# Four transformer layers and a mixed attention/SSM block on one core: new first loads, new POOL costs in the planner, a narrower rule for breaking small matmuls, and a longer search

## The chip, the cores and the metric

One Trainium2 chip, one core. The metric is the device time of one execution in microseconds, the median of several. Within the core, TensorE (PE, with its weight loads shown as PEld), VectorE (DVE), ScalarE (ACT), GpSimd (POOL) and the DMA queue that SyncE (SP) issues run beside one another and wait on semaphores.

## The reference

A sequence of 256 tokens of width 1024 goes through four layers and one further block, all in float32:

```
for i in range(4):
    hn = rms_norm(x, norm_gains[i, 0])
    m = diff_attention / stick_breaking_attention / sliding_window_sink_attention (hn)   # kinds 0, 1, 2, 0
    x = x + rms_norm(m, norm_gains[i, 1])
    f = swiglu(rms_norm(x, norm_gains[i, 2]), w_gate, w_up, w_down)                      # 1024 -> 2816 -> 1024
    x = x + rms_norm(f, norm_gains[i, 3])
xn = rms_norm_2(x, mix_norm)
z = xn @ w_in                                   # q, k, v, gate_a, u, gate_s
attn = dilated_mixture_attention(q, k, v) * silu(gate_a)
ssm  = s5_glu(u, ...) * silu(gate_s)            # 32 groups, 64 complex states each, a diagonal scan
h = x + concat(attn, ssm) @ w_out
h = h + sigmoid(rms_norm_2(h) @ w_ple_gate) * (p @ w_ple_proj)
```

Rope angles need sine and cosine of position times frequency; the SSM needs sine and cosine of its eigenvalues, and powers of them.

## The kernel before

The tokens are two blocks b of 128. A weight matrix is cut into chunks of 8 row tiles by 512 columns (2 MB). SP loads a chunk as raw tiles (three buffers of 1 MB). ACT copies it into a rounded half "hi", DVE subtracts to get "lo", and `gemm` (L726) sums three products per row tile (hi·hi, hi·lo, lo·hi), so one chunk is 24 matmuls of 512 columns for each b. The weight tiles w have eleven buffers, PSUM accumulators two for each b. The first chunk's raw tiles and the transposed input xT0 lie in the S8 ring (`S8`, L539), three buffers of 1 MB, which later holds q, k, v, the FFN accumulator and the two SSM preparation tiles pp and pt, in the order in which the program makes them. A new user of a buffer waits for the last use of the tile three places earlier: layer 1's k comes after pp.

Nothing is issued in program order. `_Program.record` (L234) keeps every instruction with a cost (`cost`, L208), its predecessors and the ring of its tiles. `schedule` (L461) then plans all engines together: `forward` (L320) is a list scheduler that starts, on the engine that is free first, the ready instruction of the lowest priority value; `backward` (L423) derives new priorities from the end. 24 tries of three passes with random settings are made, the plan with the earliest end wins, and `issue` (L491) writes the instructions out in that order, so every engine's queue is a fixed sequence. Before an activation whose function lies in another table set it issues a table load; Copy and Square need no set of their own.

What the change and the prediction touch:

- `cost`, L208: POOL's elementwise operations over n elements of each partition.
- `record`, L234: the delay put on each edge from one instruction to the next.
- `forward`, L320: with TensorE, an instruction of fewer than 100 columns is put off for a wide one when the columns of the current stretch of planned time are behind a pace; a run of instructions of one array tiling is kept together where possible.
- `setup`, L579: first loads, in the order `nc.head`; eight warm-up matmuls (`warm`, L610). After the head come the loads in `rope_tables` (L655), `prep_diff` (L960), `prep_sink` (L1116) and the block-two gains (L1618).
- `sincos`, L641: range reduction and Sin, once for the sine and once for the cosine.
- `ssm_prep_tasks`, L1291: on POOL, `coef` and `powers` are some hundred operations of 16 elements in one chain, then eight `part_e` sets of six operations of 256 elements; each ends in four transposes (tile eT) and eight small matmuls (tile ke) on TensorE. The last set's result goes out by a DMA, taps<-pp.
- `ssm_scan` and `ssm_y`, L1474 on: 128 matmuls S of 31 columns on half the array's columns, and 128 matmuls Y on a quarter of them.

All instructions of the program have the profile line L499, that of `issue`, so tiles tell them apart.

Of the kernel before, what the change touches and what calls it, by code (L numbers as in the profile page):

```python
# [10 lines left out]
F32 = mybir.dt.float32  # L11
# [61 lines left out]
CONST, COFF = _consts()  # L73

# [41 lines left out]
class _Program:  # L116
# [14 lines left out]
    DRAIN = 110.0  # L131
    window = 6
    tries, seed = 24, 346
# [74 lines left out]
    def cost(eng, method, args, kw):  # L208
# [23 lines left out]
        return 150 + (2.9 if op == ALU.mult else 3.5) * n  # L232

    def record(self, eng, method, args, kw):  # L234
# [41 lines left out]
        for o in preds.values():  # L276
            if o is not op:
                self.edge(o, op, 0.0 if o.eng == eng == "tensor" else o.lat)
# [41 lines left out]
    def forward(self, delta):  # L320
# [11 lines left out]
        while len(order) < len(self.ops):  # L332
            for e in dirty:
# [4 lines left out]
                for op in lst:  # L338
                    s = op.ready if op.ready > f else f
                    w = self.DMA[e][0] if op.call == "dma_start" else op.cost  # L340
                    if op.func is not None and self.set_of[op.func] != table:
                        w += self.SWITCH
# [18 lines left out]
                if e == "tensor" and best is not None and best.cols < 100:  # L361
# [45 lines left out]
            else:  # L407
                fin = s + op.cost
                if op.func is not None and self.set_of[op.func] != table:
                    table = self.set_of[op.func]  # L410
                    fin += self.SWITCH
# [49 lines left out]
    def schedule(self):  # L461

        self.ring_edges()
# [3 lines left out]
        self.log = []  # L467
        for i in range(self.tries):
# [8 lines left out]
            if not fresh and sigma:  # L477
                for o, z in zip(self.ops, rng.normal(0.0, sigma, len(self.ops))):
                    o.prio += z
            for _ in range(3):  # L480
                end, order = self.forward(delta)
                if best is None or end < best[0]:
                    best = (end, order, [o.start for o in self.ops])
                    self.log.append((i, round(end)))
                self.backward()
        self.end, order, starts = best
        for o, t in zip(self.ops, starts):
            o.start = t
        return order

    def issue(self, tc):  # L491
        order = self.schedule()
        table = None
        with tc.manual_schedule():
            for op in order:
# [10 lines left out]
class _Net:  # L506
# [72 lines left out]
    def setup(self):  # L579
# [3 lines left out]
        self.gT = cp.tile([P, 80], F32, name="gT")  # L583
# [6 lines left out]
        load(self.gT, a["gT"])  # L590
# [4 lines left out]
        n = len(nc.ops)  # L595
        self.prepped = 0
        if self.depth:
            self.prep(1)
        raws = [o for o in nc.ops[n:] if o.eng == "sync"]
        for b in range(NB):  # L600
            load(self.x[b], a["x"][0][b * P:(b + 1) * P, :])
        self.ident = cp.tile([P, P], F32, name="ident")
        load(self.ident, self.consts_dram[:, COFF["ident"][0]:COFF["ident"][0] + P])
        if raws:
            nc.head = [loads[1], raws[0], loads[0], raws[1], loads[2], raws[2], loads[3]] + raws[3:] + loads[4:]
        self.neghalf = cp.tile([P, 8], F32, name="neghalf")
        nc.vector.memset(self.neghalf, -0.5)
        self.warm(8)
# [32 lines left out]
    def sincos(self, sin_out, cos_out, ang, tmp):  # L641
        nc = self.nc
        for shift, dst in ((0.0, sin_out), (0.25, cos_out)):
            nc.vector.tensor_scalar(tmp, ang, 1.0 / TWO_PI, shift, op0=ALU.mult, op1=ALU.add)
            nc.vector.tensor_scalar(tmp, tmp, MAGIC, None, op0=ALU.add)
            nc.vector.tensor_scalar(tmp, tmp, MAGIC, None, op0=ALU.subtract)
            nc.vector.scalar_tensor_tensor(dst, tmp, -C1, ang, op0=ALU.mult, op1=ALU.add)
            nc.vector.scalar_tensor_tensor(dst, tmp, -C2, dst, op0=ALU.mult, op1=ALU.add)
            nc.vector.scalar_tensor_tensor(dst, tmp, -C3, dst, op0=ALU.mult, op1=ALU.add)
            if shift:  # L650
                nc.vector.tensor_scalar(dst, dst, math.pi / 2, None, op0=ALU.add)
            nc.vector.tensor_scalar(dst, dst, math.pi, -math.pi, op0=ALU.min, op1=ALU.max)
            nc.scalar.activation(dst, dst, AF.Sin)

    def rope_tables(self):  # L655
        nc, a, cp = self.nc, self.a, self.cp
        pt = self.pw(1, "post")
# [1186 lines left out]
```

## Time and profile before

| | |
|---|---|
| median of 3 runs | 1386.53 us (1385.73 to 1387.84) |
| the profiled execution | 1389.7 us |
| its span, first to last instruction | 1387.9 us |
| TensorE busy in the span | 1360.8 us |
| VectorE, ScalarE, GpSimd busy | 913.9, 766.2, 198.4 us |
| HBM | 236.90 MB read, 6.67 MB written, 175 GB/s over the span |
| mean granted TensorE clock | 0.998 |

The profiled execution is 1.8 us longer than its span, and 3.2 us above the median. TensorE's busy time is a union of modelled stretches: a matmul's stretch reaches past the start of the next, so short stops between matmuls hide in it, and a slow pace shows only in counts (matmuls in so many us). Idle time is told as the wait before an instruction, with what ended it.

### The profile page before, as it was taken

The page shows a single profiled execution, that of the slowest core. Times are in us where ns is not written, and L with a number is a line of the kernel's source. Part 1 is how long each engine was busy: PE and PEld are TensorE (multiplying, and loading weights), DVE is VectorE, ACT ScalarE, POOL GpSimd, SP SyncE. Part 2 cuts the span into 40 slices and gives each one's busy share as a digit, 9 for nine tenths or more (in the row PEclk, how much of TensorE's full clock was granted, in tenths as well). Part 3 has the DMA queues.
Part 4 walks back from the last instruction along what each step waited for, and adds up shares of the span by engine and source line. Part 5 has one row for each costly group of instructions (what it writes and reads, how often), then busy time and mean ns, then how long its engine had stood idle before and what let it go on. Part 6 is the DMA issues. An engine that isn't in the chain of part 4 may idle for free.

```text
span 1387.9 us, 17967 instructions
## 1 busy us (share of the span) xinstructions
PE 1360.8 (98%) x6820; PEld 1119.9 (81%) x6820; DVE 913.9 (66%) x1351; ACT 766.2 (55%) x1268; POOL 198.4 (14%) x331
## 2 busy tenths in 40 slices
PE   8999999999999999999999999999999999999998
PEld 5788887888888888788878888888888888887776
DVE  7986654758756655558966555598875464685583
ACT  6766554446877544446756544466664453564562
POOL 0011067603000059202000000010000000020000
PEclk9999999999999999999999999999999999999999
DMA  8553654656443566655525645554546474566550
GB/s 301 188 162 131 223 206 142 202 191 213 159 152 108 182 207 212 216 163 167 161 84 197 211 154 182 180 173 152 182 137 212 152 228 151 167 214 188 178 190 35
DMA packets 135510, 244.73 MB, mean 176 GB/s; under 512 B 6544, under 2 KB 28176, under 8 KB 135424
## 3 DMA queue, kind: packets, MB, share of 16 engines
q1 hardware_dynamic: 135424, 243.59, 53.3%
q8 instruction: 53, 0.87, 0.3%
q14 instruction: 33, 0.27, 0.1%
HBM read 236.90 MB, written 6.67 MB: 175 GB/s over the span
## 4 chain that ended last, share of the span: by engine, by line
PE 80%; DVE 8%; ACT 4%; POOL 4%; DMA 3%; issue 1%; SPq 0%; ACTq 0%; DVEq 0%; POOLq 0%
PE acc L499 70%; PE tr L499 3%; DVE w L499 3%; POOL pp L499 2%; DVE rp L499 1%; ACT w L499 1%; PE z L499 1%; PE sc L499 1%; DMA raw<-in_a_w_in_dram 1%; PE sS L499 1%; POOL pt L499 1%; PE o L499 1%; POOL q L499 1%; DMA raw<-in_w_ple_gate_dram 1%; PE Y L499 1%
## 5 line engine op out<-in xcount | busy, mean ns | idle before, releaser
L499 PE MATMUL acc<-w,hnT 128*128 128x512 f32 (+1 forms) x3552 | 837.2, 391 | 5.6 <-ACT w L499 3.1
L499 PEld LDWEIGHTS acc<-w,hnT 128*128 128x128 f32 x3552 | 653.5, 189 | 140.6 <-ACT w L499 4.2
L499 DVE TENSOR_TENSOR w<-raw,w 128x1024 fp32r<-128x1024 f32 (+1 forms) x431 | 518.9, 1218 | 185.1 <-ACT w L499 176.2
L499 ACT ACTIVATE w<-raw 128x1024 fp32r<-128x1024 f32 (+1 forms) x431 | 442.6, 1040 | 207.2 <-PE acc L499 165.9
L499 PE MATMUL acc<-w,hT 128*128 128x512 f32 x1056 | 252.0, 392 | 0.9 <-ACT hT L499 0.9
L499 PEld LDWEIGHTS acc<-w,hT 128*128 128x128 f32 x1056 | 196.0, 188 | 41.6 <-ACT hT L499 1.3
L499 PE MATMUL acc<-w,oT 128*128 128x512 f32 x480 | 120.5, 400 | 0.8 <-DVE oT L499 0.8
L499 PEld LDWEIGHTS acc<-w,oT 128*128 128x128 f32 x480 | 88.2, 188 | 19.9 <-DVE oT L499 1.2
L499 POOL TENSOR_TENSOR po_r<-po_v,neghalf 128x1 f32<-128x1 f32 x16 | 14.6, 910 | 532.0 <-DVE po_v L499 532.0
L499 DVE SCALAR_TENSOR_TENSOR sg<-acc,pn_r,sg 128x512 f32<-128x512 f32 (+1 forms) x48 | 33.8, 704 | 68.6 <-PE acc L499 49.2
L499 ACT ACTIVATE sg<-acc,pn_r 128x512 f32<-128x512 f32 (+1 forms) x48 | 31.1, 649 | 86.4 <-PE acc L499 86.4
L499 POOL TENSOR_TENSOR pg<-pg 128x128 f32<-128x128 f32 x96 | 60.6, 655 | 39.1 <-PE acc L499 35.9
L499 ACT ACTIVATE hT<-tr 128x512 fp32r<-128x512 f32 (+1 forms) x48 | 26.6, 555 | 58.6 <-PE tr L499 58.6
L499 DVE TENSOR_TENSOR hT<-tr,hT 128x512 fp32r<-128x512 f32 (+1 forms) x48 | 30.8, 641 | 24.7 <-ACT hT L499 24.7
L499 DVE TENSOR_TENSOR facc<-acc,facc 128x512 f32<-128x512 f32 x32 | 22.0, 687 | 32.8 <-PE acc L499 32.8
L499 POOL TENSOR_TENSOR pn_r<-pn_v,neghalf 128x1 f32<-128x1 f32 x20 | 16.4, 821 | 176.7 <-DVE pn_v L499 170.5
L499 ACT ACTIVATE ad_e<-sc,ad_nm 128x128 f32<-128x128 f32 (+1 forms) x64 | 26.2, 422 | 18.2 <-DVE ad_nm L499 15.3
L499 ACT ACTIVATE hnT<-gx 128x512 fp32r<-128x512 f32 x36 | 22.6, 628 | 24.4 <-DVE gx L499 24.1
L499 POOL TENSOR_TENSOR ad_r<-ad_v,neghalf 128x4 f32<-128x4 f32 x8 | 9.9, 1232 | 148.4 <-DVE ad_v L499 140.2
L499 DVE TENSOR_TENSOR hnT<-gx,hnT 128x512 fp32r<-128x512 f32 x36 | 25.2, 699 | 6.0 <-ACT hnT L499 5.7
L499 ACT ACTIVATE sqj<-x 128x512 f32<-128x512 f32 x40 | 24.9, 623 | 6.9 <-DVE x L499 6.7
L499 POOL TENSOR_TENSOR pt<-pp 128x256 f32<-128x256 f32 x32 | 25.2, 800 | 18.8 <-PE ke L499 18.2
(232 smaller groups left out, 1112.0 us busy)
## 6 DMA issues: line engine op xcount, KB each, us to landing
raw<-in_ffn_w_gate_dram SPq DMA_DIRECT2D x40, 1024.0 KB, 5.2
raw<-in_ffn_w_up_dram SPq DMA_DIRECT2D x40, 1024.0 KB, 5.1
raw<-in_ffn_w_down_dram SPq DMA_DIRECT2D x32, 1024.0 KB, 5.2
raw<-in_a_w_in_dram SPq DMA_DIRECT2D x22, 1024.0 KB, 5.2
raw<-in_ffn_w_down_dram SPq DMA_DIRECT2D x16, 768.0 KB, 4.5
raw<-in_b_w_in_dram SPq DMA_DIRECT2D x12, 1024.0 KB, 5.2
raw<-in_w_in_dram SPq DMA_DIRECT2D x12, 1024.0 KB, 5.2
raw<-in_a_w_out_dram SPq DMA_DIRECT2D x8, 1024.0 KB, 5.1
```

The costliest lines, as they stand in the source:

```text
L499: r = getattr(getattr(self.nc, op.eng), op.call)(*op.args, **op.kw)
```

## The change

- A new input "pack" (134 columns) replaces the input of the norm gains (80 columns). It also holds the positions, the rope frequencies, the two subln gains, the q and k gains and the sinks, which nine separate loads brought before.
- The head of the load queue also takes chunk 1: identity matrix, then both raw tiles of chunk 1, then x; before, x and the identity ended the head.
- 13 warm-up matmuls in place of 8.
- `issue` loads the first needed activation table ahead of everything, and the planner counts no switch for it.
- `sincos` works on sine and cosine side by side in one tile.
- POOL's cost becomes 340 + 1.85 n (multiply) or 340 + 2.8 n ns, where it was 150 + 2.9 n or 150 + 3.5 n.
- An edge from POOL to TensorE gets 3000 ns more.
- The rule that breaks small matmuls for wide ones holds only when TensorE's current tiling is the full array.
- The search has 60 tries of three passes (24 before), another seed, and then 120 single passes that put noise on the priorities within one stretch of 20, 60 or 150 us of the best plan and keep what does not end later.

The diff, cut to its core:

```diff
+PACK = 134
...
+    SPARE = 3000.0
...
-    tries, seed = 24, 346
+    tries, local, seed = 60, 120, 3
...
-        return 150 + (2.9 if op == ALU.mult else 3.5) * n
+        return 340 + (1.85 if op == ALU.mult else 2.8) * n
...
-                self.edge(o, op, 0.0 if o.eng == eng == "tensor" else o.lat)
+                lag = 0.0 if o.eng == eng == "tensor" else o.lat
+                self.edge(o, op, lag + self.SPARE if (o.eng, eng) == ("gpsimd", "tensor") else lag)
...
-                    if op.func is not None and self.set_of[op.func] != table:
+                    if op.func is not None and self.set_of[op.func] != table is not None:
...
-                if e == "tensor" and best is not None and best.cols < 100:
+                if e == "tensor" and best is not None and best.cols < 100 and mode in (None, (P, P)):
...
+                    fin += self.SWITCH if table is not None else 0.0
...
-                    fin += self.SWITCH
...
+        def attempt(i, delta):
+            nonlocal best
+            prio = [o.prio for o in self.ops]
+            end, order = self.forward(delta)
+            if best is None or end <= best[0]:
+                if best is None or end < best[0]:
+                    self.log.append((i, round(end)))
+                best = (end, order, np.array([o.start for o in self.ops]), np.array(prio), (delta, self.stick, self.pace))
...
-                end, order = self.forward(delta)
-                if best is None or end < best[0]:
-                    best = (end, order, [o.start for o in self.ops])
-                    self.log.append((i, round(end)))
+                attempt(i, delta)
...
-        self.end, order, starts = best
-        for o, t in zip(self.ops, starts):
+        for i in range(self.tries, self.tries + self.local):
+            width, sigma = rng.choice((20e3, 60e3, 150e3)), rng.choice((100.0, 300.0, 1000.0, 3000.0))
+            centre = rng.uniform(0.0, best[0])
+            delta, self.stick, self.pace = best[4]
+            near = np.abs(best[2] - centre) < width / 2
+            prio = np.where(near, best[2 + rng.integers(2)] + rng.normal(0.0, sigma, n), best[3])
+            for o, x in zip(self.ops, prio.tolist()):
+                o.prio = x
+            attempt(i, delta)
+        self.end, order, starts = best[:3]
+        for o, t in zip(self.ops, starts.tolist()):
...
-        table = None
+        table = next((self.set_of[op.func] for op in order if op.func is not None), None)
...
+            if table:
+                self.nc.scalar.preload_act_table_set(table)
...
-        self.gT = cp.tile([P, 80], F32, name="gT")
+        self.pack = cp.tile([P, PACK], F32, name="pack")
+        self.gT = self.pack[:, 0:80]
...
-        load(self.gT, a["gT"])
+        load(self.pack, a["pack"])
...
-        if self.depth:
-            self.prep(1)
-        raws = [o for o in nc.ops[n:] if o.eng == "sync"]
+        raws = [[], []]
+        for i in range(2 if self.depth else 0):
+            n = len(nc.ops)
+            self.prep(i + 1)
+            raws[i] = [o for o in nc.ops[n:] if o.eng == "sync"]
+        self.ident = cp.tile([P, P], F32, name="ident")
+        load(self.ident, self.consts_dram[:, COFF["ident"][0]:COFF["ident"][0] + P])
...
-        self.ident = cp.tile([P, P], F32, name="ident")
-        load(self.ident, self.consts_dram[:, COFF["ident"][0]:COFF["ident"][0] + P])
-        if raws:
-            nc.head = [loads[1], raws[0], loads[0], raws[1], loads[2], raws[2], loads[3]] + raws[3:] + loads[4:]
+        if self.depth:
+            r0, r1 = raws
+            nc.head = [loads[1], r0[0], loads[0], r0[1], loads[2], r0[2], loads[3]] + r0[3:] + loads[4:5] + r1[:2]
+            nc.head += loads[5:] + r1[2:]
...
-        self.warm(8)
+        self.warm(13)
...
-    def sincos(self, sin_out, cos_out, ang, tmp):
+    def sincos(self, out, ang, tmp):
...
-        for shift, dst in ((0.0, sin_out), (0.25, cos_out)):
-            nc.vector.tensor_scalar(tmp, ang, 1.0 / TWO_PI, shift, op0=ALU.mult, op1=ALU.add)
-            nc.vector.tensor_scalar(tmp, tmp, MAGIC, None, op0=ALU.add)
-            nc.vector.tensor_scalar(tmp, tmp, MAGIC, None, op0=ALU.subtract)
-            nc.vector.scalar_tensor_tensor(dst, tmp, -C1, ang, op0=ALU.mult, op1=ALU.add)
-            nc.vector.scalar_tensor_tensor(dst, tmp, -C2, dst, op0=ALU.mult, op1=ALU.add)
-            nc.vector.scalar_tensor_tensor(dst, tmp, -C3, dst, op0=ALU.mult, op1=ALU.add)
-            if shift:
-                nc.vector.tensor_scalar(dst, dst, math.pi / 2, None, op0=ALU.add)
-            nc.vector.tensor_scalar(dst, dst, math.pi, -math.pi, op0=ALU.min, op1=ALU.max)
-            nc.scalar.activation(dst, dst, AF.Sin)
+        for i in range(2):
+            nc.vector.tensor_scalar(tmp[:, i], ang, 1.0 / TWO_PI, 0.25 * i, op0=ALU.mult, op1=ALU.add)
+        nc.vector.tensor_scalar(tmp, tmp, MAGIC, None, op0=ALU.add)
+        nc.vector.tensor_scalar(tmp, tmp, MAGIC, None, op0=ALU.subtract)
+        nc.vector.scalar_tensor_tensor(out, tmp, -C1, ang[:, None, :].to_broadcast(list(out.shape)), op0=ALU.mult,
+                                       op1=ALU.add)
+        nc.vector.scalar_tensor_tensor(out, tmp, -C2, out, op0=ALU.mult, op1=ALU.add)
+        nc.vector.scalar_tensor_tensor(out, tmp, -C3, out, op0=ALU.mult, op1=ALU.add)
+        nc.vector.tensor_scalar(out[:, 1], out[:, 1], math.pi / 2, None, op0=ALU.add)
+        nc.vector.tensor_scalar(out, out, math.pi, -math.pi, op0=ALU.min, op1=ALU.max)
+        nc.scalar.activation(out, out, AF.Sin)
...
-        pt = self.pw(1, "post")
-        inv, pos = pt[:, 0:32], pt[:, 32:32 + NB]
-        posi = self.pw(1, "posi")[:, :NB].bitcast(I32)
-        o, n = COFF["inv"]
-        nc.sync.dma_start(out=inv, in_=self.consts_dram[:, o:o + n])
-        nc.sync.dma_start(out=posi, in_=a["positions"][0].rearrange("(b p) -> p b", p=P))
-        nc.vector.tensor_copy(pos, posi)
+        inv = self.pack[:, 82:114]
+        pos = self.pw(1, "pos")[:, :NB]
+        nc.vector.tensor_copy(pos, self.pack[:, 80:82].bitcast(I32))
...
-        self.sincos(sc[:, :64], sc[:, 64:128], ang[:, :64], tmp[:, :64])
+        two = lambda t: t[:, :128].rearrange("p (t n) -> p t n", t=2)
+        self.sincos(two(sc), ang[:, :64], two(tmp))
...
-        gcol = self.small(1, "gcol")
-        nc.sync.dma_start(out=gcol, in_=a["a_subln"][inst].rearrange("(p o) -> p o", o=1))
+        gcol = self.pack[:, 114 + inst:115 + inst]
...
-        sk = self.small(16, "sink")
-        nc.sync.dma_start(out=sk, in_=a["c_sinks"][inst].partition_broadcast(P))
+        sk = self.pack[:, 118:134]
...
-            mag, ai_, ar_, num, den, cr, ci, t1, t2 = (cols(16) for _ in range(9))
+            mag, num, den, cr, ci, t1 = (cols(16) for _ in range(6))
+            trig, t2 = (cols(32).rearrange("p (t g) -> p t g", t=2) for _ in range(2))
+            ai_, ar_ = trig[:, 0], trig[:, 1]
...
-            self.sincos(ai_, ar_, t1, t2)
+            self.sincos(trig, t1, t2)
...
-                for key, src, sc in (("gq", "q_norm_2", 0.125), ("gk", "k_norm_2", 1.0)):
-                    g = self.small(1, key)
-                    for h in range(2):
-                        nc.sync.dma_start(out=g[64 * h:64 * h + 64, :], in_=a[src][0].rearrange("(p o) -> p o", o=1))
-                    if sc != 1.0:
-                        g2 = self.small(1, key + "s")
-                        nc.vector.tensor_scalar(g2, g, sc, None, op0=ALU.mult)
-                        g = g2
-                    st[key] = g
+                st["gk"] = self.pack[:, 117:118]
+                st["gq"] = self.small(1, "gqs")
+                nc.vector.tensor_scalar(st["gq"], self.pack[:, 116:117], 0.125, None, op0=ALU.mult)
...
+    two = lambda v: np.tile(v[0], 2)[:, None]
+    pack = [rows.transpose(2, 0, 1).reshape(P, 80), i["positions"][0].reshape(NB, P).T.astype(np.int32).view(np.float32),
+            CONST[:, COFF["inv"][0]:COFF["inv"][0] + 32], i["a_subln"].T, two(i["q_norm_2"]), two(i["k_norm_2"]),
+            np.broadcast_to(i["c_sinks"][0], (P, 16))]
...
-        "gT": rows.transpose(2, 0, 1).reshape(P, 80),
+        "pack": np.concatenate(pack, axis=1),
...
```

## Rows read from the trace of the kernel before

**Rows 1.** The page, busy time of each engine and its share of the span.
```profile
PE 1360.8 (98%) x6820; PEld 1119.9 (81%) x6820; DVE 913.9 (66%) x1351; ACT 766.2 (55%) x1268; POOL 198.4 (14%) x331
```

**Rows 2.** Busy time by stretch: each engine, granted clock, DMA share, GB/s.
```profile
9.00:12.00 3.00, 3.00 (x9) 2.29 (x8) 2.63 (x7) 3.00 (x9) 0.00 (x0) 1.00 1.04 405
13.00:16.00 3.00, 3.00 (x15) 2.47 (x14) 3.00 (x6) 3.00 (x8) 0.00 (x0) 1.00 1.06 347
...
25.00:72.00 47.00, 46.30 (x231) 37.64 (x230) 46.02 (x83) 30.68 (x69) 0.00 (x0) 1.00 0.56 189
...
227.00:239.00 12.00, 9.49 (x34) 7.59 (x33) 3.24 (x7) 2.39 (x3) 8.50 (x16) 0.72 0.26 101
239.00:1255.00 1016.00, 1011.24 (x4966) 836.25 (x4965) 668.44 (x906) 566.54 (x911) 133.26 (x181) 1.00 0.54 176
1255.00:1345.00 90.00, 84.83 (x625) 68.60 (x625) 58.29 (x128) 45.45 (x71) 2.00 (x2) 1.00 0.56 180
```

**Rows 3.** The timeline of the first 26 us: start, length, what, wait before it.
```profile
0.98 3.59 PE L499 MATMUL warm<-warm 128*128 128x512 bf16 x8 [0.98 <-DVE neghalf L499]
...
5.10 1.28 ACT L499 ACT_TABLE_LOAD   x1 [5.10 <-DMA gT<-in_gT_dram]
...
7.66 14.01 PE L499 MATMUL acc<-w,hnT 128*128 128x512 f32 x50 [3.08 <-ACT w L499]
...
11.91 1.71 SPq L499 DMA_DIRECT2D raw<-in_a_w_in_dram  x2
...
20.45 0.48 DVE L499 SCALAR_TENSOR_TENSOR angs<-angt,angs 128x64 f32<-128x64 f32 x2
20.81 1.28 ACT L498 ACT_TABLE_LOAD   x1
...
22.77 1.22 DVE L499 TENSOR_TENSOR w<-raw,w 128x1024 fp32r<-128x1024 f32 x1
...
24.04 2.33 PE L499 MATMUL acc<-w,hnT 128*128 128x512 f32 x9 [2.38 <-DVE w L499]
```

**Rows 4.** Groups of POOL's instructions, costliest first: busy, mean ns, idle before.
```profile
L499 POOL TENSOR_TENSOR pt<-pp 128x256 f32<-128x256 f32 x32 | 25.2, 800 | 18.8 <-PE ke L499 18.2
L499 POOL TENSOR_TENSOR pp<-pp 128x16 f32<-128x16 f32 x57 | 18.7, 355 | 43.0 <-DMA pp<-in_ssm_dram 35.4 <-DVE pp L499 4.6 <-ACT pp L499 2.5
```

**Rows 5.** The timeline of POOL, 172 to 245 us.
```profile
210.34 1.20 POOL L499 TENSOR_TENSOR pp<-pp 128x16 f32<-128x16 f32 x1
...
221.18 0.22 POOL L499 TENSOR_TENSOR pp<-q 128x16 f32<-128x16 f32 x1
```

**Rows 6.** The timeline of TensorE, 200 to 250 us.
```profile
229.31 0.33 PE L499 MATMUL eT<-ident,pt 128*128 128x128 f32 x1 [1.26 <-POOL pt L499]
230.89 0.90 PE L499 MATMUL eT<-ident,pt 128*128 128x128 f32 x3 [1.25 <-POOL pt L499]
...
233.15 6.44 PE L499 MATMUL acc<-w,hnT 128*128 128x512 f32 x18
```

**Rows 7.** The timeline of TensorE, 1255 us to the end.
```profile
1257.85 0.89 PE L499 MATMUL S<-ssm,scrE 128*64 128x31 f32 x24
...
1259.10 0.30 PE L499 MATMUL S<-ssm,scrE 128*64 128x31 f32 x2
...
1306.89 0.27 PE L499 MATMUL sS<-m_causal,identb 128*128 128x256 bf16 x1 [1.62 <-ACT ssm L499]
...
1371.20 11.04 PE L499 MATMUL acc<-w,hnT 128*128 128x512 f32 x48
1382.08 1.29 PE L499 MATMUL acc<-w,pT 128*128 128x512 f32 x5
```

**Rows 8.** The timeline around the first k of layer 1.
```profile
340.54 0.34 SPq L499 DMA_DIRECT2D taps<-pp  x1
...
346.45 0.58 ACT L499 ACTIVATE k<-tr 128x512 f32<-128x512 f32 x1
```

**Rows 9.** DMA issues by line: KB each, median us from issue to landing.
```profile
taps<-pp SPq DMA_DIRECT2D x1, 256.0 KB, 4.3
```

More of the change, by code (lines that the diff above doesn't have):

```diff
@@ L467, in schedule @@
         self.log = []
+        n = len(self.ops)
+        def attempt(i, delta):
[6 more added lines that the diff above has]
+                best = (end, order, np.array([o.start for o in self.ops]), np.array(prio), (delta, self.stick, self.pace))
         for i in range(self.tries):
@@ L477, in schedule @@
             if not fresh and sigma:
-                for o, z in zip(self.ops, rng.normal(0.0, sigma, len(self.ops))):
+                for o, z in zip(self.ops, rng.normal(0.0, sigma, n)):
                     o.prio += z
             for _ in range(3):
-                end, order = self.forward(delta)
-                if best is None or end < best[0]:
-                    best = (end, order, [o.start for o in self.ops])
-                    self.log.append((i, round(end)))
+                attempt(i, delta)
                 self.backward()
-        self.end, order, starts = best
-        for o, t in zip(self.ops, starts):
+        for i in range(self.tries, self.tries + self.local):
[9 more added lines that the diff above has]
+        for o, t in zip(self.ops, starts.tolist()):
             o.start = t
@@ L594, in setup @@
             load(xs[:, k:k + m].rearrange("p k b q -> p (k b q)"), a["xT"][:, k * 256:(k + m) * 256])
-        n = len(nc.ops)
         self.prepped = 0
-        if self.depth:
-            self.prep(1)
-        raws = [o for o in nc.ops[n:] if o.eng == "sync"]
+        raws = [[], []]
[5 more added lines that the diff above has]
+        load(self.ident, self.consts_dram[:, COFF["ident"][0]:COFF["ident"][0] + P])
         for b in range(NB):
             load(self.x[b], a["x"][0][b * P:(b + 1) * P, :])
-        self.ident = cp.tile([P, P], F32, name="ident")
-        load(self.ident, self.consts_dram[:, COFF["ident"][0]:COFF["ident"][0] + P])
-        if raws:
-            nc.head = [loads[1], raws[0], loads[0], raws[1], loads[2], raws[2], loads[3]] + raws[3:] + loads[4:]
+        if self.depth:
+            r0, r1 = raws
+            nc.head = [loads[1], r0[0], loads[0], r0[1], loads[2], r0[2], loads[3]] + r0[3:] + loads[4:5] + r1[:2]
+            nc.head += loads[5:] + r1[2:]
         self.neghalf = cp.tile([P, 8], F32, name="neghalf")
         nc.vector.memset(self.neghalf, -0.5)
-        self.warm(8)
+        self.warm(13)
     def warm(self, n):
```

## The prediction, made before the changed kernel ran

> **What bounds the kernel.** I read the page first: TensorE is busy 1360.8 of 1387.9 us [rows 1], so only its own stops and its slow stretches can be won, and every other engine matters only where it makes TensorE late. Next the table by stretch [rows 2], for where those stops are. From 239 to 1255 us TensorE lacks 4.8 us in 1016; the rest lies in three places: the first 72 us, 227 to 239 us, and from 1255 us on. Counts tell the pace: 48 full matmuls in 11.04 us late in the run [rows 7] are 0.227 us each (less the last one's 0.39 us of length, over 47 starts).
>
> In the first place the timeline [rows 3] shows the warm-up matmuls ending at 4.57 us, the first real matmul at 7.66 us, and a stop of 2.38 us before 24.04 us. Its 50 matmuls take 14.01 us, where 50 at 0.227 us take 11.4 us. Nine stand in 9 to 12 us against fifteen in 13 to 16 us [rows 2]: the first ones go at little more than half the later pace, as the eight warm-up matmuls do (3.59 us, up to 0.45 each) [rows 3]. VectorE is busy 46.0 of the 47 us from 25 to 72 us [rows 2], so that is where the start is held next.
>
> In the second place two transposes of the SSM preparation wait 1.26 and 1.25 us for POOL's tile pt [rows 6]. After these stops the granted clock is 0.72 over 227 to 239 us [rows 2], which is 6.7 of 12 us at 1.2 instead of 2.4 GHz, and 18 matmuls take 6.44 us [rows 6]. In the third place TensorE lacks 5.2 us in 90 [rows 2], in waits such as 1.62 us for the gelu [rows 7], and the span goes on for 4.5 us behind the last matmul (1383.4 to 1387.9 us) [rows 7].
>
> **The change, part by part.** The sum goes against the profiled execution's 1389.7 us; the median lies 3.2 us under it.
>
> Table load at the start. ACT loads its table at 5.10 us, when the gains have landed, for 1.28 us, and the first matmul waits for ACT's w [rows 3]. Loaded ahead, it lies beside the transfers. The pack has 27 KB more than the gains, under 0.1 us at 405 GB/s [rows 2]. Term: 1.2 us off; the ends are 0 and 1.3.
>
> Warm-up. Five more matmuls at up to 0.45 us [rows 3] end by 6.8 us. The first real matmul can then start at 6.4 us, so they cost 0.4 us at most, and TensorE does not stop between. No row shows when the clock then rises. If no sooner than before, counted from the first real matmul, nothing is won; if before it, the whole 2.2 us by which 11.4 us plus the first small waits fall short of 14.01 us. I take 1.5 us with that cost taken off, nearer to the upper end, because TensorE is then at work throughout instead of stopping for 3.08 us [rows 3]. The Trainium skill, "TensorE: Matmul & The Clock Gate", Part 1, says that the slow level is the default and that sustained matmul work releases it; by that alone the term would be the whole 2.2 us and the sum 0.7 us lower.
>
> Second chunk. Its raw loads go out at 11.91 us, after x, the identity and three small ones; ACT then loads a table at 20.81 us and VectorE makes the first w at 22.77 us [rows 3]. In the new queue they go out at about 5 us. With xT, chunk 0 and the second chunk's first half, 4.2 MB have to move at 347 to 405 GB/s [rows 2], so that half lands near 12.5 us, before TensorE has used up chunk 0 (6.4 + 48 x 0.227 = 17.3 us). The stop of 2.38 us should go. Of the small loads, nine leave SP's queue. They are costed at nothing: behind the head, raw loads wait for one of three buffers, which VectorE's w frees; if that cover goes, each is one issue of SP, about as long as a raw load's (two in 1.71 us [rows 3]). `sincos` drops from 15 to 9 VectorE operations and one activation: six at 0.24 us [rows 3] are 1.4 us, less 0.5 us for 64 more columns in seven others at 1.2 ns a column (1.22 us for 1024 [rows 3]): 0.9 us of VectorE's time. What is late next: x lands some 5.6 us later (2.1 MB at 376 GB/s, the mean of the two rates), its squares and the rope factors after it, to about 24 us; the rope of chunk 0 is needed when TensorE wants that accumulator back, two chunks on, at 28 us. That covers it by 4 us. VectorE does not cover: saturated to 72 us, it can be finished sooner only by its earlier start (1.3 us), the 0.9 us of `sincos` and its own idle time (about 1 us in 47 [rows 2]). So of 1.2 + 1.5 + 2.4 us I keep 4.2 for the three, that is 1.5 us for this one; ends 0 and 2.5.
>
> POOL's costs. A 16-column operation took 355 ns on average, a 256-column multiply 800 [rows 4]. The old formula gives 196 and 892, the new one 370 and 814. With 99 short ones in the chain (57 of pp [rows 4], and 42 of q8), the plan had POOL some 15 us early, and put transposes where nothing was ready. The new costs and the 3 us of spare take TensorE to other work meanwhile. The stops of 2.5 us and half of 6.7 us at the lower level go: 5.9 us. I take 5.5; ends 0 and 5.9. The spare touches nothing else, for no other TensorE instruction waited for POOL.
>
> Small matmuls. S stands in six runs, broken five times for wide matmuls; 24 S in a row take 0.82 us to the next start, two take 0.23 us [rows 7], so a return costs 0.23 - 2 x 0.034 = 0.16 us. All of them: 0.8 us; I take 0.5, ends 0 and 0.8. Y ran unbroken, and ke fills the array, where the rule stays.
>
> Search. It draws the whole order anew. It can reach the idle time of 72 to 1345 us outside the POOL stop, about 4.8 + 5.2 + 1 us [rows 2], and can open a stop of the POOL kind (5.9 us) where none is. I take 1.6 us off, with 8 off and 6 on as ends.
>
> Sum: 1.2 + 1.5 + 1.5 + 5.5 + 0.5 + 1.6 = 11.8 us. 1389.7 - 11.8 = 1377.9 us for such an execution, **1374.7 us** for the median.
>
> **The rivals.** *VectorE keeps the start.* For it speaks its 98% from 25 to 72 us; against it, the stop at 24 us is VectorE's order, not its load. The 4.2 us are lost: 1378.9 us.
>
> *POOL stays late.* Its 16-column operations take 0.22 us, or 1.20 us at times [rows 5], and 1.2 us is the length of VectorE's w operation [rows 3]. So POOL's real cost is set by how many w operations fall into the chain, not by n; with ten more than before it is 10 us late and the spare is used up. The 5.5 us come back as a stop elsewhere: 1380.2 us. The Trainium skill, "SBUF — State Buffer", "Who interferes with whom", has this rule: the two engines share a port pair, and whichever of a POOL operation and a VectorE operation with two SBUF inputs starts second waits for the other's end. Rows 5 agree.
>
> *The SSM sets run into layer 1 (slower).* Layer 1's k needs pp's buffer: the last DMA from it is issued at 340.54 us, and k is written at 346.45 us [rows 8]. That DMA lands 4.3 us after its issue [rows 9], which leaves 1.6 us. POOL is now planned longer, and each set by 3 us of spare, so the last sets may come later. A set takes six operations, some 5 us at 0.80 [rows 4] or a little more. One set late costs 5 - 1.6 = 3.4 us; two, 8.4 us, and with half of 6.7 us of lower clock behind such a stop 11.8 us, no gain at all; from three on it is slower, 13.4 + 3.4 = 16.8 us: 1391.5 us. Against it: TensorE has other chunks, and the plan knows the buffers.
>
> *No effect on balance.* The new order gives back at the end, and in mode changes, what the three places win: 1386.5 us.
>
> **How the numbers follow.** Chances: forecast 0.56, VectorE 0.13, POOL late 0.12, unchanged 0.08, slower 0.11. A measurement of this kernel can tell 0.2%, 2.8 us, from no change: the first three lie below 1383.7 us, so faster 0.81, same 0.08, slower 0.11. The low end takes all terms at their best: 1.3 + 2.2 + 2.5 + 5.9 + 0.8 + 8 = 20.7 us, 1366 us. The high end, 1387 us, takes in the three milder rivals and leaves out the slower one.
>
> **What would show it.** First real matmul near 6.4 us with no stop after the warm-up; w of the second chunk before the squares of x; no matmul waiting for pt, and the clock at 1.00 from 25 us to the end; S in fewer runs; POOL's 16-column mean still near 0.36 us. A wait on POOL or a stretch of low clock anywhere, or a first k of layer 1 behind taps, would make it wrong.

## The result, and the profile after

The changed kernel took 1373.1 us in the median of four runs (1371.86 to 1374.33), the kernel before 1387.02 beside it: a ratio of 0.990, 95% interval 0.9883 to 0.9918. The profiled execution took 1374.15 us, 15.55 less than that of before; its span is 1372.3 us, 15.6 less. Of that difference 1.6 us come from the two executions profiled: that of before lies 2.7 us above its median, that of the changed kernel 1.1 us.

The page, busy time of each engine; it answers to [rows 1]:

```profile
PE 1356.4 (99%) x6825; PEld 1119.8 (82%) x6825; DVE 910.8 (66%) x1339; ACT 769.2 (56%) x1269; POOL 204.9 (15%) x331
```

TensorE's busy time fell by 4.4 us; the other 11.2 us of the span were idle time. The view of waits says whose. Its columns are who waited for what: total us, times, longest. First the largest of TensorE's waits in the kernel before, then those in the changed one:

```profile
PE acc L499 <- DVE w L499: 3.4, 3, 2.4
PE acc L499 <- ACT w L499: 3.1, 1, 3.1
PE eT L499 <- POOL pt L499: 2.5, 2, 1.3
PE acc L499 <- ACT pT L499: 1.7, 1, 1.7
PE sS L499 <- ACT ssm L499: 1.6, 1, 1.6
...
```

```profile
PE S L522 <- DMA scrE<-scrE: 2.3, 1, 2.3
PE acc L522 <- ACT w L522: 1.3, 1, 1.3
...
```

All rows of this view add up to 22.3 us before and 11.5 us after. By stretches: 7.1 to 4.1 us up to 72 us, 2.5 to nothing from 222 to 246 us, 6.8 to 2.8 us from 1200 us on, 5.8 to 4.6 us in all the rest. The waits on w at the start and on POOL's pt are down or gone. One is new: 2.3 us for scrE.

Busy time by stretch of the changed kernel (PE, PEld, DVE, ACT, POOL, each with its count; then clock, DMA share, GB/s); the third to fifth and seventh rows answer to [rows 2]:

```profile
12.00:16.00 4.00, 4.00 (x11) 3.15 (x11) 4.00 (x12) 3.11 (x7) 1.90 (x4) 0.57 1.06 381
...
25.00:72.00 47.00, 45.71 (x228) 36.99 (x227) 41.10 (x77) 28.28 (x66) 1.02 (x1) 1.00 0.56 188
227.00:239.00 12.00, 12.00 (x59) 9.91 (x58) 7.69 (x10) 6.03 (x7) 11.06 (x29) 1.00 0.57 187
239.00:1248.00 1009.00, 1003.23 (x5009) 831.15 (x5007) 659.10 (x912) 560.49 (x907) 139.62 (x188) 1.00 0.53 176
1248.00:1255.00 7.00, 7.00 (x71) 5.72 (x68) 2.42 (x5) 3.84 (x5) 1.64 (x1) 0.52 0.82 284
1255.00:1345.00 90.00, 89.47 (x548) 74.34 (x547) 68.08 (x129) 55.63 (x79) 2.98 (x2) 1.00 0.49 167
```

From 227 to 239 us TensorE has no idle time, 59 matmuls instead of 34, and the full clock. There are two new stretches at the lower level: 12 to 16 us, where the eleven matmuls take the time of more than seventeen, and 1248 to 1255 us, behind the new wait.

The timeline of the first 45 us (start, length, what, wait before it), against [rows 3]:

```profile
0.72 1.28 ACT L517 ACT_TABLE_LOAD   x1 [0.72 <-PEq L1852]
...
0.98 5.19 PE L522 MATMUL warm<-warm 128*128 128x512 bf16 x13 [0.98 <-DVE neghalf L522]
...
5.82 3.40 PE L522 MATMUL acc<-w,hnT 128*128 128x512 f32 x12
...
6.46 1.81 SPq L522 DMA_DIRECT2D raw<-in_a_w_in_dram  x2
...
9.44 1.06 ACT L522 ACTIVATE w<-raw 128x1024 fp32r<-128x1024 f32 x1 [0.32 <-DMA raw<-in_a_w_in_dram]
...
10.55 0.73 PE L522 MATMUL acc<-w,hnT 128*128 128x512 f32 x2 [1.33 <-ACT w L522]
...
11.81 20.49 PE L522 MATMUL acc<-w,hnT 128*128 128x512 f32 x82 [0.53 <-DVE w L522]
```

The table load lies beside the transfers, the first real matmul starts at 5.82 us instead of 7.66, the second chunk's raw loads go out at 6.46 us instead of 11.91, and 82 matmuls follow one another from 11.81 us on, so the stop of 2.38 us before 24 us is gone. But at 10.55 us TensorE waits 1.33 us for ACT's w, which itself waited for its raw tile: the first chunk's own transfers hold it now.

The timeline from 1233 us on, where the before kernel had S in six runs [rows 7]:

```profile
1238.21 5.73 SPq L522 DMA_DIRECT2D scrE<-scrE  x3
...
1242.22 2.06 PE L522 MATMUL S<-ssm,scrE 128*64 128x31 f32 x64
...
1244.21 1.19 PE L522 MATMUL acc<-w,hnT 128*128 128x512 f32 x4
...
1247.70 2.62 PE L522 MATMUL S<-ssm,scrE 128*64 128x31 f32 x48 [2.30 <-DMA scrE<-scrE]
...
1250.26 2.08 PE L522 MATMUL acc<-w,hnT 128*128 128x512 f32 x4
...
1252.26 1.07 PE L522 MATMUL S<-ssm,scrE 128*64 128x31 f32 x16
```

S is in three runs now, and the second one wants scrE before it has landed. The stop and what follows it, 7 us at 0.52, cost 2.3 and about 3.4 us. Even so the last run of five pT matmuls starts at 1366.61 us instead of 1382.08 [rows 7], 15.5 us earlier.

POOL's groups (busy, mean ns, idle before), against [rows 4]:

```profile
L522 POOL TENSOR_TENSOR pt<-pp 128x256 f32<-128x256 f32 x32 | 28.9, 914 | 42.3 <-PE ke L522 41.6
...
L522 POOL TENSOR_TENSOR pp<-pp 128x16 f32<-128x16 f32 x57 | 20.8, 395 | 38.5 <-DMA pp<-in_ssm_dram 30.5 <-DVE pp L522 4.3 <-ACT pp L522 3.5
```

POOL is no faster, a little slower in fact (800 to 914 ns, 355 to 395 ns). What changed is that it waits 41.6 us for ke, which are TensorE's matmuls, where it waited 18.2: now POOL is ahead.

### The profile page after: what moved, and what is told of

It is laid out like the page before. It is cut to its first block, busy times and chain, and to the rows that moved or that the text cites. A ratio compares the mean times of both kernels' runs of the same rounds, so it can differ in the third digit from the quotient of the medians.

```text
span 1372.3 us, 17953 instructions
## 1 busy us (share of the span) xinstructions
PE 1356.4 (99%) x6825; PEld 1119.8 (82%) x6825; DVE 910.8 (66%) x1339; ACT 769.2 (56%) x1269; POOL 204.9 (15%) x331
## 4 chain that ended last, share of the span: by engine, by line
PE 89%; DVE 6%; DMA 2%; ACT 1%; issue 1%; POOL 0%; SPq 0%; ACTq 0%; DVEq 0%
PE acc L522 77%; PE tr L522 3%; DVE w L522 2%; PE z L522 1%; PE sS L522 1%; PE sc L522 1%; DVE rp L522 1%; DMA raw<-in_a_w_in_dram 1%; PE o L522 1%; DVE q L522 1%; PE Y L522 1%; PE asT L522 1%; PE oB L522 0%; PE oC L522 0%; DMA raw<-in_w_ple_gate_dram 0%
## 5 line engine op out<-in xcount | busy, mean ns | idle before, releaser
L522 POOL TENSOR_TENSOR pt<-pp 128x256 f32<-128x256 f32 x32 | 28.9, 914 | 42.3 <-PE ke L522 41.6
```

The costliest lines, as they stand in the source:

```text
L522: r = getattr(getattr(self.nc, op.eng), op.call)(*op.args, **op.kw)
```

## The experiments

The time moved by about as much as I had said. Open were the start's terms one by one, whether POOL's term belongs to the costs or to the new order, and how much of the rest is the search. Any edit of a cost or of the program draws the whole order anew, so some kernels keep the changed kernel's order and touch only what is issued, and others are planned anew; these I compare as groups too. Every kernel computes the whole reference; the two on the warm-up change only how many warm-up matmuls are issued. Each ratio is to runs of the kernel before on the same chip.

**The start, with the order kept.** First the table load that the program asks for ahead of everything, taken out:

```diff
-            if table:
-                self.nc.scalar.preload_act_table_set(table)
+            table = None
```

> The changed kernel with its order of instructions kept and only the early table load taken out, so that the first load stands behind ACT's first wait again and one more load comes before the first Exp. My sum's term: the first real matmul moves from 5.8 to about 7.1 us and the time grows by 1.2 us. Rival (the start is bound by transfers and w): the matmuls of chunk 0 already stop 1.5 and 0.7 us for w at 8.8 and 10.9 us in the changed kernel, so a later start only fills these stops, and the time grows by 0 to 0.4 us.

It took 1374.03 us, 0.9901 [0.9885, 0.9916]. But the edit did not move what it was meant to move. ACT's timeline of this kernel:

```profile
0.72 1.28 ACT L521 ACT_TABLE_LOAD   x1 [0.72 <-PEq L1851]
...
25.44 1.28 ACT L520 ACT_TABLE_LOAD   x1
```

The first load still stands at 0.72 us, as in the changed kernel, though the program no longer asks for it there. All that the edit did was to add one load, at 25.44 us. So a_nopre does not test the term of 1.2 us; redrawn kernels with the old start do, further down.

Then five warm-up matmuls skipped, and nine more issued:

```diff
+                if op.eng == "tensor" and "warm" in op.args[0].tensor.name:
+                    nw += 1
+                    if 2 <= nw <= 6:
+                        continue
```

> The changed kernel with its order kept and 8 warm-up matmuls issued instead of 13. My sum's term: the first real matmuls go at the lower clock and the time grows by 1.5 us. Rival: in the changed kernel the clock rises at 5.6 us, falls again after the stops at 8.8 and 10.9 us, and 8 matmuls then go at the lower level; with 8 warm-ups the first 12 real ones are slow and use up the waiting time instead, so the time stays within 0.5 us or even falls by 1 to 1.7 us.

```diff
+                warm = op.eng == "tensor" and "warm" in op.args[0].tensor.name
+                for _ in range(10 if warm and not op.kw["start"] and not op.kw["stop"] and not self.warmed else 1):
```

> The changed kernel with its order kept and 22 warm-up matmuls. They should end near 8 us, so that the first 12 real matmuls run until w of the third row tile is there at 10.6 us, without a stop. If the stop and the fall of the clock behind it cost what the trace shows (8 matmuls at 0.43 instead of 0.227 us), the time falls by about 1.7 us. If the start is bound by w alone and the clock costs nothing, it stays within 0.3 us; if TensorE was needed before 8 us, it grows by up to 2 us.

They took 1372.72 us, 0.9896 [0.9881, 0.9912], and 1374.9 us, 0.9911 [0.9895, 0.9927]. TensorE's timeline from the start, of a_nopre, with 8 and with 22 warm-ups:

```profile
0.98 5.73 PE L521 MATMUL warm<-warm 128*128 128x512 bf16 x13 [0.98 <-DVE neghalf L521]
6.15 3.35 PE L521 MATMUL acc<-w,hnT 128*128 128x512 f32 x12
10.91 0.73 PE L521 MATMUL acc<-w,hnT 128*128 128x512 f32 x2 [1.41 <-ACT w L521]
```

```profile
0.98 3.59 PE L527 MATMUL warm<-warm 128*128 128x512 bf16 x8 [0.98 <-DVE neghalf L527]
5.81 4.79 PE L527 MATMUL acc<-w,hnT 128*128 128x512 f32 x12 [1.24 <-ACT hnT L527]
11.16 0.73 PE L527 MATMUL acc<-w,hnT 128*128 128x512 f32 x2 [0.56 <-ACT w L527]
12.42 17.80 PE L527 MATMUL acc<-w,hnT 128*128 128x512 f32 x76 [0.53 <-DVE w L527]
```

```profile
0.98 7.20 PE L525 MATMUL warm<-warm 128*128 128x512 bf16 x22 [0.98 <-DVE neghalf L525]
7.83 3.10 PE L525 MATMUL acc<-w,hnT 128*128 128x512 f32 x12
11.38 0.73 PE L525 MATMUL acc<-w,hnT 128*128 128x512 f32 x2 [0.46 <-ACT w L525]
12.64 17.55 PE L525 MATMUL acc<-w,hnT 128*128 128x512 f32 x75 [0.53 <-DVE w L525]
```

In a_nopre the first real matmul comes 0.33 us later (6.15 against 5.82) with the table load in the same place, so this shift is not the load's. With 8 warm-ups the first twelve go much slower (4.79 us against 3.40), yet what they lose is then not waited for: 0.56 us before the next pair instead of 1.33. In all four kernels that pair waits for ACT's w, and ACT had waited for the raw tile (0.32 us in the changed kernel, 0.34, 0.35 and 0.75 in these), with the DMA share at 0.91 to 0.93 from 6 to 11 us. From 12 to 16 us all three keep the full clock with 15 or 16 matmuls, where the changed kernel has 0.57 and 11. By 40 us the changed kernel has done 117 acc matmuls, these 116, 118 and 119: within 0.7 us. So the pace of TensorE in the first 10 us is worth nothing that can be measured, in either direction.

**The start as a whole, on the old planner.** The changed kernel, with the planner's costs, spare, rule and search put back:

```diff
-    SPARE = 3000.0
+    SPARE = 0.0
-    tries, local, seed = 60, 120, 3
+    tries, local, seed = 24, 0, 346
-        return 340 + (1.85 if op == ALU.mult else 2.8) * n
+        return 150 + (2.9 if op == ALU.mult else 3.5) * n
-                if e == "tensor" and best is not None and best.cols < 100 and mode in (None, (P, P)):
+                if e == "tensor" and best is not None and best.cols < 100:
```

> The changed kernel's loads, warm-up, first table load and joined sine and cosine with the planner of before (old POOL costs, no spare, old rule for small matmuls, 24 tries, no local search, old seed). By my sum the start is worth 4.2 us, by the trace of the changed kernel 2.4 us: 1383 to 1385 us, and the wait for pt should stand again with its 6 us. Rival (redrawing): the start is 2 to 3 us earlier, and the rest moves by several microseconds either way.

It took 1391.48 us, 1.0022 [1.0011, 1.0033]: slower than before, with the better start in it. Its stretch from 222 to 246 us, beside TensorE's timeline there:

```profile
222.00:246.00 24.00, 20.62 (x96) 17.27 (x95) 13.56 (x19) 8.74 (x11) 18.45 (x34) 0.86 0.35 114
```

```profile
228.25 0.90 PE L522 MATMUL eT<-ident,pt 128*128 128x128 f32 x3 [3.38 <-POOL pt L522]
```

The POOL stop is back, longer than before (3.38 us in one piece). What the start itself is worth can be read across all kernels, because up to 160 us nothing waits for the SSM preparation: the number of acc matmuls done by then. The four orders with the old start have 505, 507, 511 and 512, the ten kernels with the new one 520 to 539, b_start 522 among them; these ten are seven orders, since a_nopre, a_warm8 and a_warm22 share that of the changed kernel. The rows of acc alone, of before, of the best old start (before with another seed), of the changed kernel and of the poorest new start (the changed kernel with the short search):

```profile
0.00:160.00 160.00, 126.30 (x511) 95.74 (x512) 14.68 (x22) 7.56 (x15) 1.00 0.61 203
```

```profile
0.00:160.00 160.00, 127.23 (x512) 95.56 (x513) 14.68 (x22) 7.57 (x15) 0.99 0.59 199
```

```profile
0.00:160.00 160.00, 130.23 (x524) 97.56 (x525) 14.69 (x22) 7.58 (x15) 0.99 0.58 202
```

```profile
0.00:160.00 160.00, 128.08 (x520) 97.14 (x521) 14.53 (x22) 7.53 (x15) 0.99 0.61 208
```

The groups do not overlap. At 0.227 us each [rows 7], 524 against 511 are 3.0 us; the means of the groups, 524.4 and 508.8, are 3.5 us apart. That is an estimate, since an order may put other matmuls off meanwhile.

The orders with the old start also say which part of it counts. In b_pool, b_seed3 and b_long, whose loads, warm-up and issuing are those of the kernel before, the first table load stands at 0.72 us and not at 5.10 (ACT's first activation there is w from the raw tile, in the kernel before it is hnT, which waits for the gains), and the first real matmul at 5.83 to 5.96 us instead of 7.66. Still they have done 96 to 108 acc matmuls by 40 us, where the kernel before has 114. So the earlier table load and the earlier first matmul are worth nothing that these counts show. What all four orders have is a stop for w of the second chunk, as in b_seed3:

```profile
5.96 2.06 PE L499 MATMUL acc<-w,hnT 128*128 128x512 f32 x6 [1.39 <-ACT hnT L499]
...
22.04 0.73 PE L499 MATMUL acc<-w,hnT 128*128 128x512 f32 x2 [0.65 <-ACT w L499]
24.70 5.54 PE L499 MATMUL acc<-w,hnT 128*128 128x512 f32 x16 [1.93 <-DVE w L499]
```

These waits, from 22 to 26 us, add up to 2.38 us in the kernel before and to 2.58, 3.09 and 3.46 us in b_seed3, b_pool and b_long. In all ten kernels with the new start TensorE runs without a wait from 12.7 us or sooner to 30 us.

**POOL's costs.** Alone on the kernel before, and taken out of the changed one:

```diff
-        return 150 + (2.9 if op == ALU.mult else 3.5) * n
+        return 340 + (1.85 if op == ALU.mult else 2.8) * n
-                self.edge(o, op, 0.0 if o.eng == eng == "tensor" else o.lat)
+                self.edge(o, op, 0.0 if o.eng == eng == "tensor" else o.lat + 3000.0 * ((o.eng, eng) == ("gpsimd", "tensor")))
```

> The kernel before with two edits of the planner alone: POOL's new cost formula and the 3 us of spare between POOL and TensorE; same search, same seed. My theory: no transposes wait for pt, no lower clock near 230 us, and the time falls by 4 to 6 us, to about 1381 to 1383 us. Rival (redrawing): the wait goes, since any redrawn order may miss it, but the rest of the order is drawn anew as well, and the time lands anywhere within 5 us of before.

```diff
-    SPARE = 3000.0
+    SPARE = 0.0
-        return 340 + (1.85 if op == ALU.mult else 2.8) * n
+        return 150 + (2.9 if op == ALU.mult else 3.5) * n
```

> The changed kernel with POOL's old cost formula and no spare, planned anew by the same long search. My theory: transposes of the SSM preparation wait for pt again, with a stretch of lower clock behind them, and the time grows by 4 to 6 us. Rival: the longer search or the redrawn order won these microseconds, not the costs; then no such wait stands and the time stays within 2 us of the changed kernel's.

They took 1385.69 us, 0.9986 [0.9972, 1.0], and 1378.54 us, 0.9936 [0.9919, 0.9952]. From 222 to 246 us, first before, then before with the new costs:

```profile
222.00:246.00 24.00, 21.49 (x96) 17.73 (x95) 10.80 (x16) 8.56 (x11) 13.78 (x35) 0.86 0.34 113
```

```profile
222.00:246.00 24.00, 24.00 (x117) 20.05 (x116) 13.42 (x16) 11.38 (x13) 11.74 (x41) 1.00 0.55 185
```

The stop of 2.5 us and 0.14 of 24 us of clock (3.4 us) are gone: 5.9 us. Yet the whole kernel gained some 2 us only. Its redrawn order had 505 acc matmuls by 160 us instead of 511. At 1180 us it was 32 ahead of before (7.3 us), and its span ended 3.9 us sooner, so the tail lost another 3.4 us. In the other direction the old costs brought only a wait of 0.17 us on pt back, at full clock. The 5 us that a_poolold lost against the changed kernel are in the range of my theory, but they are not its stop. So the old costs open the stop in some orders only: over 2 us in two of five (before and b_start), 0.2 and 0.3 us in two, none in one. With the new costs it was in none of the six orders planned with them.

b_pool alone cannot tell the costs from a new draw, for b_seed3 has lost the stop with no cost changed. The two groups can: in all five orders with the old costs a transpose or its weight load waits for pt (0.6 to 7.1 us in all, both counted), in none of the six with the new ones, and the first transpose starts at 211.4 to 221.3 us in the five, at 222.8 to 244.5 us in the six. Which of the two edits does it, the cost formula or the spare, is not shown, since they were always changed together.

**The seed and the search.** Before with seed 3; the changed kernel with the short search and the old seed; before with the long search; the changed kernel's long search with the old seed:

```diff
-    tries, seed = 24, 346
+    tries, seed = 24, 3
```

> The kernel before with nothing changed but the seed of its search (3 for 346). If the old costs make the wait for pt, transposes wait again 2 us or more and the time stays within 3 us of before. If that wait was the luck of one order, it is gone here, and the time moves by several microseconds either way; this run is the measure of what redrawing alone does.

```diff
-    tries, local, seed = 60, 120, 3
+    tries, local, seed = 24, 0, 346
```

> The changed kernel with the search of before: 24 tries, no local search, old seed; costs, spare, rule and start stay changed. If the long search carries the part of the gain that my sum did not name (some 4 us), the time is 4 to 6 us over the changed kernel's, about 1377 to 1379 us. If the named parts carry it, the time stays within 2 us of the changed kernel's.

```diff
-    tries, seed = 24, 346
+    tries, local, seed = 60, 120, 3
+            near = np.abs(best[2] - centre) < width / 2
+            prio = np.where(near, best[2 + rng.integers(2)] + rng.normal(0.0, sigma, n), best[3])
...
```

> The kernel before with the search alone changed: 60 tries, 120 single passes with noise in short stretches, seed 3; loads, costs, spare and rule as before. If the search is the larger part, as the 7 us between the changed kernel and its short search say, the time falls by 5 to 9 us, to about 1379 to 1383 us, mostly behind 1240 us and in the attention layers, while the first 220 us stay as they were. If the search only pays with the new costs, it stays within 4 us of before, and transposes may wait for pt.

```diff
-    tries, local, seed = 60, 120, 3
+    tries, local, seed = 60, 120, 346
```

> The changed kernel with another seed (346) of the same long search. If the long search settles near one value, the time is within 2 us of the changed kernel's 1373 us; if 1373 us is one good draw, it lies 3 to 7 us above, as with the old POOL costs (1378.5 us) and the short search (1380.1 us).

In this order: 1383.8 us, 0.9964 [0.995, 0.9978]; 1380.1 us, 0.9936 [0.9923, 0.9949]; 1382.96 us, 0.9968 [0.9955, 0.998]; 1386.12 us, 0.9985 [0.9975, 0.9995]. The last is the one that tells most: the same graph, costs and number of tries, another seed, and by the ratios 11.8 of the 13.9 us are gone. TensorE's timeline and the table of stretches show where some of it went:

```profile
1346.86 0.66 PE L522 MATMUL tr<-ident,x 128*128 128x128 f32 x4 [1.60 <-DVE x L522]
1349.54 1.22 PE L522 MATMUL acc<-w,pT 128*128 128x512 f32 x2 [2.02 <-ACT pT L522]
```

```profile
1340.00:1356.00 16.00, 12.38 (x48) 9.54 (x47) 12.21 (x17) 7.42 (x12) 2.94 (x2) 0.79 0.40 147
```

Two stops of 1.60 and 2.02 us and 0.21 of 16 us of clock (3.4 us) make 7 us in this place. There is another low stretch near 340 us. On before, the other seed (1383.8) and the long search with that same seed (1382.96) do about the same, and on the changed graph with seed 346 the long search (0.9985) came out slower than the short one (0.9936). So no run shows that the longer search wins anything by its length.

**The rule for small matmuls, and more spare.** The old rule in the changed kernel, and the spare put on loads that SP issues for TensorE too:

```diff
-                if e == "tensor" and best is not None and best.cols < 100 and mode in (None, (P, P)):
+                if e == "tensor" and best is not None and best.cols < 100:
```

> The changed kernel with the old rule for small matmuls, planned anew. My sum says 0.5 us slower, by S in about six runs instead of three. Rival one: the unbroken runs of S are what stands before the stop of 2.3 us for scrE at 1247 us and the lower clock behind it, so the old rule takes that stop away and the time falls by up to 5 us. Rival two (redrawing): any value within 5 us.

```diff
-                self.edge(o, op, lag + self.SPARE if (o.eng, eng) == ("gpsimd", "tensor") else lag)
+                self.edge(o, op, lag + self.SPARE if (o.eng, eng) in (("gpsimd", "tensor"), ("sync", "tensor")) else lag)
```

> The changed kernel with the 3 us of spare also on edges from a load to TensorE, that is on the tiles that TensorE reads as loaded (scrE, scrM, scrG). The changed kernel, the one with the old POOL costs and the one with the short search all wait about 2 us for scrE or scrM between 1247 and 1266 us. If the planner's too early landing makes these waits, they go here, the clock stays up behind 1240 us, and the time falls by 3 to 5 us, to about 1368 to 1370 us. If the redrawing rules, it lands anywhere within 5 us of the changed kernel's.

They took 1375.01 us, 0.9915 [0.99, 0.9929], and 1371.96 us, 0.9889 [0.9873, 0.9905]. With the old rule S stands in ten runs, with a wait of only 0.41 us on scrE and no low clock behind it. The time differs from the changed kernel's by less than a seed does, so the rule's own worth is not shown. With the wider spare, S:

```profile
1247.66 2.99 PE L522 MATMUL S<-ssm,scrE 128*64 128x31 f32 x96
1254.22 1.12 PE L522 MATMUL S<-ssm,scrE 128*64 128x31 f32 x32
```

```profile
1240.00:1265.00 25.00, 25.00 (x238) 20.77 (x238) 14.56 (x43) 14.29 (x24) 3.27 (x2) 1.00 0.74 236
```

No wait, full clock, with 96 S in one run. The stop before 1247.70 us was a wait for a load, as its row says, and slack for that load in the plan took it away; this is one order, and a_narrowold, without that slack, has only 0.41 us of it too. The whole kernel has the lowest time of all, but its interval overlaps that of the changed kernel, so it can't be called faster. Waits of 1.14 us at 919 us and 0.94 us at 975 us took part of the win.

## Why the prediction was right

The total held: 1374.7 us said, 1373.1 measured, and 11.8 us named against 13.9 between the medians and 15.6 between the two profiled executions. That it came so close is in part luck: the same change with another seed of its search took 1386.12 us. By its own steps:

- *The start, 4.2 us:* 3.0 to 3.5 us by the counts. Its parts were wrong. The table load, taken at 1.2, is worth nothing that the counts show (b_pool, b_seed3, b_long; a_nopre did not move it). The warm-up, taken at 1.5, is worth nothing in the changed kernel (a_warm8, a_warm22). My argument there was TensorE's pace, but a faster pace only brings TensorE sooner to a w whose raw tile has not landed. The Trainium skill, "TensorE: Matmul & The Clock Gate", Part 1, says that sustained work releases the slow level; by that alone the warm-up would have been worth 2.2 us. The trace agrees on the pace (the twelve matmuls take 3.40, 4.79 and 3.10 us behind 13, 8 and 22 warm-ups, though the column of the granted clock shows 1.00 from 6 to 11 us in all three), not on a gain. Nearly all of the start's gain is then the second chunk's loads with the smaller edits around them (`sincos`, the pack), which I took at 1.5; these were not tried one by one. Also, I had bounded the three terms by VectorE at 1.3 + 0.9 + 1 = 3.2 us and kept 4.2 without saying why; the counts lie at the bound.
- *POOL's costs, 5.5 us:* right in place and mechanism, and in size for the kernel before as it was planned: 5.9 us from 222 to 246 us, gone in b_pool and in all orders with the new costs. As a worth of the old costs in general it is too much, for three of five orders with them stop 0.3 us or less. The rival that POOL stays late did not come, though POOL did grow slower, as that rival said; the spare and the larger costs outweighed it.
- *Small matmuls, 0.5 us:* S went to three runs as said, but S costs 5.8 us of busy time now against 5.0 before, because part of it runs at the lower level (4.1 us in a_dmaspare, at full clock). The step that failed is that nothing was said of scrE: an unbroken run wants its loads sooner. That is 2.3 us of waiting and some 3.4 us of pace, against 0.8 us at best; the row of the wait names the load, and in a_dmaspare it is gone.
- *Search, 1.6 us, ends 8 off and 6 on:* what the start and POOL leave of 15.6 is 6.2 to 6.7 us, 1.6 of them by the choice of executions. Some 4.5 us of it come behind 1180 us, where the changed kernel is 49 acc matmuls ahead (11.1 us), even with the new stop. The term was sized too small by 3 to 5 us, within its ends; the two errors, on the start and here, lie on opposite sides. But it is a draw and not a property of the search: the same search with the old seed gives 1386.12 us. What share of it would come again is open, with two long draws of the changed graph only, 1373.1 and 1386.12.
- *The slower rival:* its place was the right one to look at. The last DMA from pp goes out at 336.81 us and ACT's k, at 340.13 us, now waits 0.71 us for it, where there was slack before [rows 8]; no set came late and TensorE did not wait. *VectorE keeps the start* did not come either: 3.0 to 3.5 of the 4.2 us were won, VectorE has 41.1 us of work from 25 to 72 us instead of 46.0, and the start is held by w in the first 12 us instead.
- *"The clock at 1.00 from 25 us to the end"* failed, at 1248 us.

Parts alone did not add up. By the ratios, POOL's costs alone gave 1.9 us, the long search alone 4.4, the start alone cost 3.1, and all together gave 13.9. The whole kernel's time holds the change's parts plus a draw of the order, and the draw moved it by up to 12 us with nothing else changed.

## What to carry to other kernels

Where a planner writes the order, read a part's worth in its own stretch (waits, clock and counts there), over several redrawn orders, and don't take it from the total: one seed can be worth nearly as much as the whole change. Give slack in the plan to every edge into the engine that bounds the kernel whose delay varies, and look at what an unbroken run wants sooner. Before paying for a faster first stretch, look at what the engine waits for next: if that is a transfer, the pace ahead of it is free to lose. After an edit that takes something out, look in the trace whether it is gone: here the table load stood where it had stood.

## What was not expected of the hardware

A stop of 2.30 us of TensorE cost more behind it than itself: from 1248 us the clock fell to 0.52 over 7 us, about the lower level throughout, of which half is lost. Falls of the same kind stand behind 3.38 us at 228 us in b_start and behind 1.60 and 2.02 us near 1347 us in a_long346. But in the kernel before two waits of 1.7 and 1.6 us, for pT and the gelu, had none behind them, so the length of one wait does not decide it. Nor do like waits always end alike: in the changed kernel the clock fell at 12 us behind 1.33 and 0.53 us with two matmuls between, and in a_nopre it stayed at 1.00 behind 1.41 and 0.53. In the same order, from 1250 to 1255 us, it was 0.50 in a_nopre behind two waits for scrE of 1.37 and 0.24 us, and 1.00 in a_warm22 behind two of 1.24 and 0.56. Nor does each execution have these falls: of the changed kernel's, one had a mean clock of 1.000 and took 1372.05 us, the profiled one 0.996 and 1374.15 us, and one 0.997 and 1371.86 us, so the total does not simply grow by the pace lost in a stretch. In four of the fourteen kernels profiled no stretch fell between the warm-up and the last matmuls (a_poolold, b_pool, a_narrowold, a_dmaspare), and b_pool among them took 1385.69 us: the clock explains single stretches here, not the ranking.
